# A macaron block on one core: the last squares summed on VectorE, the closing norm in pieces, and two VectorE differences moved in the mixer

## The chip, the cores and the metric

The kernel runs on one NeuronCore of a Trainium2 chip. The metric is the device time of one execution in microseconds. Three runs of the kernel before took 916.35, 917.20 and 917.82 us; the median is 917.2. The engines are TensorE (PE, with PEld for its weight loads), VectorE (DVE), ScalarE (ACT), GpSimd (POOL) and SyncE (SP), which issues most of the transfers. POOL issues those that add to what lies at their destination.

## What is computed

One layer: a half feed-forward, a token mixer, a second half feed-forward, and a closing RMS norm over 1024 features of 512 tokens, all in float32.

```python
def rmsnorm(x, g):
    x32 = x.astype(jnp.float32)
    y = x32 * lax.rsqrt(jnp.mean(x32 * x32, axis=-1, keepdims=True) + EPS)
    return (y * g.astype(jnp.float32)).astype(x.dtype)

def swiglu(x, w_gate, w_up, w_down):
    return (jax.nn.silu(x @ w_gate) * (x @ w_up)) @ w_down

x = x + 0.5 * swiglu(rmsnorm(x, ffn1_norm[layer]), ...)
x = x + token_mixer(rmsnorm(x, mix_norm[layer]), w_in[layer], w_out[layer], ...)
x = x + 0.5 * swiglu(rmsnorm(x, ffn2_norm[layer]), ...)
...
return rmsnorm(x, final_norm)
```

The token mixer projects to queries, keys and values, runs four heads of differential attention and eight heads of dilated attention, and projects back.

## The kernel before, in words

Activations lie transposed, features on the partitions: `x[0]` to `x[7]` are 128 features by 512 tokens each. A float32 product is made of three products of rounded parts: every operand is cast on ScalarE to a high half (a CAST row), and VectorE takes the rest (a subtraction that writes the low half); TensorE adds high by high, high by low and low by high (`mm3`, L141 to L143).

**The mixer** is a list of pieces of TensorE work ("chunks"), in the order `plan` = v0 q0 q1 v1 q2 q3 q4 v2 q5 q6 v3 q7, eight chunks for each name. `q0` to `q7` are the projections of eight attention units (units 0 to 3 differential, 4 to 7 dilated); each makes a query tile `pq` and a key tile `pk` in PSUM. Work of the other engines is put at a chunk with a rank: `put(t, rank, f)`. Ranks below 10 are emitted before the products of chunk `t`, ranks of 10 and more behind them; within one side smaller ranks come first. TensorE, VectorE and ScalarE execute in exactly the order in which the program was emitted, so these numbers set the order on each engine. SP and POOL are ordered by a scheduler.

When the projection of a unit is done (chunk `e`), its two tiles are scaled (`tq`, `tk`) and turned into score operands: `q0`, `q1` hold queries and their rests on the two halves of the partitions; `k0`, `k1` the keys, and `l0`, `l1` the rests of the keys. There are three ways. Units 0 and 7 are done at once (`evac_now`). Units 1 to 4 cast in `evac_q` at chunk `e`, and in `evac_k` at `e + 1` copy halves by SP's transfers, take the rests of the keys (L1051) and then the rests of the queries (L1054). Units 5 and 6 cast the whole key tile (`cast_k`, L1083), take its rest `kl` (`low_k`, L1089), and send both to the four places by four transfers each on SP's queue (`send`, L1078).

The attention of a unit starts some five chunks behind its projection. A score (`score`, L1191 and L1192) is two products into one of only two PSUM tiles tagged `s`; VectorE then adds the bias strip and finds the row's extreme in one custom instruction (L1194, `pr<-sc,strip`), which frees the PSUM tile, and ScalarE takes the exponential (L1197). For units 0 to 3 the finished head is turned, scaled into a high half `mh` (ScalarE, L1272) and a low half `ml` (VectorE, L1291), and POOL adds both into one tile `mx` by transfers (L1285, L1286). The weights of the projections are split as they come: cast on ScalarE (L916), rest on VectorE (L920).

**The end.** The second feed-forward closes with down projections by blocks: four units of seven steps (`SEVEN`), each step 12 products of 128 x 256, which yield two features' tiles at a time from sums and differences. In the last unit (`x[6]`, `x[7]`) the steps run as `LAST_SEVEN`: a11, s3, s2, a12, a22, s1, s4. Behind a step, `down_step` updates a half of `x[6]` or `x[7]` (L461), and `last` is called for the closing norm. The squares of `x[0]` to `x[5]` have been summed in `sq` before; the squares of `x[6]` and `x[7]` go to `q6`, `q7` (tiles `sql`) on ScalarE, by halves of 256 tokens (`left`, `right`).

The closing norm works by halves of the tokens. `final_means(hh)` takes the column means of the squares with 128 x 1 products (`st_n`, L1666), here over three sources (`sq`, `q6`, `q7`) and two blocks of 128 tokens; ScalarE takes the root (L1669), VectorE the reciprocal and a step of refinement (L1670 to L1674) and two diagonal tiles (`dgl`, L1677). `final_spread(hh)` spreads the factors over the partitions with one product (`bcl`, L1681), and `final_out` multiplies eight tiles (L1691) and sends them out in pairs on SP's queue. `final_end` runs at the last step: the spread of the left half, one pair of results, means and factors of the right half, the other three pairs, then the right half.

Of the kernel before, what the change touches and what calls it, by code (L numbers as in the profile page):

```python
# [21 lines left out]
P = 128  # L22
S = 512
# [59 lines left out]
def tile_macaron(ctx: ExitStack, tc, xs, xT, wf, wgu1, wst1, wd1, wdg1, wqk, wv, wo, wgu2, wst2, wd2,  # L83
# [922 lines left out]
    def qk_chunks(u):  # L1006
# [34 lines left out]
        def evac_k():  # L1041
            q0, q1, k0, k1, l0, l1 = qk[u]
            tq, tk = st["tq"], st["tk"]

            def other_half(t, a, b):
                nc.sync.dma_start(t[b, :].bitcast(F32), t[a, :].bitcast(F32))

            other_half(k0, lo, hi)
            other_half(k1, hi, lo)
            for a, b, kx, lx in ((lo, hi, k0, l0), (hi, lo, k1, l1)):  # L1050
                V.tensor_tensor(lx[a, :], tk[a, :], kx[a, :].bitcast(F32), op=ALU.subtract)  # L1051
                other_half(lx, a, b)
            for a, b, qx in ((lo, hi, q0), (hi, lo, q1)):
                V.tensor_tensor(qx[b, :], tq[a, :], qx[a, :].bitcast(F32), op=ALU.subtract)  # L1054
# [19 lines left out]
        elif u in SPREAD:  # L1074
# [28 lines left out]
            put(e + 2, 11, low_k)  # L1103
# [3 lines left out]
        else:  # L1107
            put(e, 11, evac_q)
            put(e + 1, 11, evac_k)
        return [lambda k=k: chunk(k) for k in range(KD)]  # L1110
# [531 lines left out]
    def last(t, o, put):  # L1642


        left, right = slice(0, HS), slice(HS, S)
        if o == "s3":
            fin["sq"] = [slot(4 + i, f"sql{i}") for i in range(2)]
        q6, q7 = fin["sq"]
        for name, n, q, c in (("a12", KD - 2, q6, left), ("a22", KD - 1, q7, left),
                              ("s1", KD - 1, q7, right), ("s4", KD - 2, q6, right)):  # L1650
            if o == name:
                put(t, A.activation, q[:, c], x[n][:, c], AF.Square)
        if o == "s3":
            put(t, A.activation, root[:], eps[:], AF.Sqrt)
        elif o == "s1":
            put(t, final_means, 0)
# [3 lines left out]
    def final_means(hh):  # L1660
        ps = pp.tile([P, S], F32, tag="mm", name=f"st_n4{hh}", bufs=4)
        n = NQ // 2
        for i in range(n):
            c = slice((hh * n + i) * P, (hh * n + i + 1) * P)
            for q, src in enumerate((sq, *fin["sq"])):
                T.matmul(ps[:, i:i + 1], src[:, c], ones_d[:, 0:1], start=q == 0, stop=q == 2)  # L1666
        y = sp.tile([P, n], F32, tag="yt4", name=f"ly{hh}", bufs=2)
        t = sp.tile([P, n], F32, tag="mx", name=f"lt{hh}", bufs=3)
        A.activation(y[:], ps[:, :n], AF.Sqrt, bias=eps[:])  # L1669
# [6 lines left out]
        for i in range(n):  # L1676
            V.tensor_scalar_mul(dg[:, i * P:(i + 1) * P], ident[:], y[:, i:i + 1])  # L1677

    def final_spread(hh):
        pb = fin["pb", hh] = pp.tile([P, S], F32, tag="mm", name=f"bcl{hh}", bufs=4)  # L1680
        T.matmul(pb[:, :HS], ones_m[:], fin["dg", hh][:, :HS], start=True, stop=True)  # L1681

    def final_out(hh, pairs):
        c = slice(hh * HS, (hh + 1) * HS)
        pb = fin["pb", hh]
        for g2 in pairs:
            y = cp.tile([P, S], F32, tag=f"xh{hh * 4 + g2}", name=f"y{hh}{g2}")
            y2 = y[:].rearrange("p (m q) -> p m q", m=2)
            for j in range(2):
                m = 2 * g2 + j  # L1690
                V.scalar_tensor_tensor(y2[:, j, :], x[m][:, c], sm[:, 3 * KD + m:3 * KD + m + 1],  # L1691
                                       pb[:, :HS], op0=ALU.mult, op1=ALU.mult)
                if hh == 1 and g2 == KD // 2 - 1:
                    nc.sync.dma_start(out[m * P:(m + 1) * P, c], y2[:, j, :])
            if hh == 0 or g2 < KD // 2 - 1:
                nc.sync.dma_start(
                    out[2 * g2 * P:(2 * g2 + 2) * P, c].rearrange("(m p) q -> p m q", p=P), y2)

    def final_end():
        final_spread(0)  # L1700
        final_out(0, range(1))
        final_means(1)
        final_out(0, range(1, 4))
        final_spread(1)
        final_out(1, range(4))
# [111 lines left out]
```

## Time and profile before

| | |
|---|---|
| median of three runs | 917.2 us (916.35 to 917.82) |
| the profiled execution | 916.25 us |
| its span, first to last instruction | 914.5 us |
| mean granted TensorE clock | 0.996 |
| VectorE busy | 758.5 us, 83% |
| ScalarE busy | 546.0 us, 60% |
| transfers | 147.39 MB, mean 161 GB/s |

How to read the rows that follow: a row of the timeline gives start and duration in us, the engine, the line of the kernel, the operation, output and inputs by the program's names, the shape, and how many instructions of the kind follow each other. In brackets stands how long the engine had been idle before, and what ended that. SPq is the queue of SyncE, on which an instruction only issues a transfer. Several rows of one matmul in float32 are its passes.

### The profile page before, as it was taken

Reading aid. Unit: us, or ns where it says so; the run is one execution under the profiler, and the core shown is the slowest. Engines: PE = TensorE matmul, PEld = TensorE weight load, DVE = VectorE, ACT = ScalarE, POOL = GpSimd, SP = SyncE. Lnnn points to the kernel's source line nnn. Section 1 sums busy time; section 2 is a strip of 40 time slices with the busy share of each in tenths; the row PEclk is TensorE's granted clock in tenths of the full one; section 3 lists DMA queues with packets and bytes.
Section 4 is the critical chain, followed back from the end, with each engine's and each line's share of the span. In section 5 each row is a group of like instructions: output and inputs, shape, how many; then the busy total and the mean of one; then the engine's idle time right before and its main releaser. Section 6 shows DMA issues by size and latency. Waiting matters only on the chain.

```text
span 914.5 us, 17685 instructions
## 1 busy us (share of the span) xinstructions
PE 901.4 (99%) x6565; PEld 844.2 (92%) x6565; DVE 758.5 (83%) x1601; ACT 546.0 (60%) x1149; POOL 112.4 (12%) x142
## 2 busy tenths in 40 slices
PE   9999999999999999999999999999999999999995
PEld 7889999999999998988979889889999899999995
DVE  7699997677998994779887859999899678798796
ACT  7356674455765764666756848456667345666462
POOL 1011101012103100000000320011110111220100
PEclk9999999999999999999999999999999999999998
DMA  8456756578758742446364674556673857984732
GB/s 277 114 161 151 175 138 180 141 202 214 196 150 206 198 148 73 115 131 162 102 178 121 187 156 112 169 159 150 171 210 93 218 146 192 221 203 123 199 112 92
DMA packets 66598, 147.39 MB, mean 161 GB/s; under 512 B 7712, under 2 KB 10016, under 8 KB 66512
## 3 DMA queue, kind: packets, MB, share of 16 engines
q1 hardware_dynamic: 48672, 113.29, 38.4%
q0 software_dynamic: 17840, 32.98, 22.0%
q8 instruction: 51, 0.84, 0.4%
q14 instruction: 35, 0.29, 0.1%
HBM read 137.28 MB, written 2.14 MB: 152 GB/s over the span
## 4 chain that ended last, share of the span: by engine, by line
PE 93%; DVE 4%; ACT 2%; DMA 1%; issue 1%; SPq 0%; DVEq 0%; ACTq 0%
PE pv L985 2%; PE pv L987 2%; PE pv L986 2%; PE po L1232 2%; PE pdb L142 1%; PE pda L142 1%; PE pda L143 1%; PE pdb L143 1%; PE pda L141 1%; PE pdb L141 1%; PE pga L143 1%; PE pua L143 1%; PE pua L142 1%; PE pua L141 1%; PE pga L141 1%; PE pga L142 1%
## 5 line engine op out<-in xcount | busy, mean ns | idle before, releaser
L1197 ACT ACTIVATE pr<-pr,small 128x128 f32<-128x128 f32 (+3 forms) x64 | 36.0, 563 | 37.5 <-DVE small L1194 37.0
L420 ACT CAST w<-s2b 128x512 fp32r<-128x512 f32 x52 | 32.4, 624 | 22.8 <-DVE s2b L402 22.5
L420 ACT CAST w<-s2a 128x512 fp32r<-128x512 f32 x48 | 29.9, 624 | 22.4 <-DVE s2a L402 21.6
L1194 DVE CUSTOM_DVE_ANT_0 pr<-sc,strip 128x128 f32<-128x128 f32 (+3 forms) x64 | 30.7, 485 | 11.2 <-PE sc L1192 11.0
L424 DVE TENSOR_TENSOR w<-s2b,w 128x512 fp32r<-128x512 f32 x52 | 35.7, 687 | 1.6 <-ACT w L420 1.1
L985 PE MATMUL pv<-w,xh 128*128 128x256 f32 x128 | 36.0, 282 | 0.0
L986 PE MATMUL pv<-w,xl 128*128 128x256 f32 x128 | 35.8, 280 | 0.0
L987 PE MATMUL pv<-w,xh 128*128 128x256 f32 x128 | 35.7, 279 | 0.0
L424 DVE TENSOR_TENSOR w<-s2a,w 128x512 fp32r<-128x512 f32 x48 | 33.0, 687 | 1.0 <-ACT w L420 0.7
L141 PE MATMUL pq<-xh,w 128*128 128x512 f32 x64 | 26.5, 414 | 0.0
L920 DVE TENSOR_TENSOR w<-raw_qk,w 128x512 fp32r<-128x512 f32 x32 | 21.6, 686 | 5.6 <-ACT w L916 5.6
L142 PE MATMUL pq<-xl,w 128*128 128x512 f32 x64 | 25.2, 393 | 0.0
L141 PE MATMUL pk<-xh,w 128*128 128x512 f32 x64 | 25.1, 392 | 0.0
L143 PE MATMUL pq<-xh,w 128*128 128x512 f32 x64 | 25.0, 391 | 0.0
L142 PE MATMUL pk<-xl,w 128*128 128x512 f32 x64 | 25.0, 391 | 0.0
L143 PE MATMUL pk<-xh,w 128*128 128x512 f32 x64 | 25.0, 391 | 0.0
L985 PEld LDWEIGHTS pv<-w,xh 128*128 128x128 f32 x128 | 24.1, 188 | 0.3
L986 PEld LDWEIGHTS pv<-w,xl 128*128 128x128 f32 x128 | 24.1, 188 | 0.2
L987 PEld LDWEIGHTS pv<-w,xh 128*128 128x128 f32 x128 | 24.1, 189 | 0.0
L916 ACT CAST w<-raw_qk 128x512 fp32r<-128x512 f32 x32 | 19.4, 615 | 7.3 <-issue 4.2
L1191 PE MATMUL sc<-k,q 128*128 128x256 f32 (+2 forms) x64 | 23.2, 363 | 0.4 <-DVE small L1194 0.4
L1232 PEld LDWEIGHTS po<-v,ptb 128*128 128x128 f32 x160 | 21.6, 191 | 1.7
(835 smaller groups left out, 4093.0 us busy)
## 6 DMA issues: line engine op xcount, KB each, us to landing
raw_qk<-wqk_dram SPq DMA_DIRECT2D x16, 512.0 KB, 3.4
raw0bg<-wst_dram SPq DMA_DIRECT2D x9, 512.0 KB, 4.3
raw0bu<-wst_dram SPq DMA_DIRECT2D x9, 512.0 KB, 5.5
raw_gua<-wgu_dram SPq DMA_DIRECT2D x8, 512.0 KB, 3.7
raw0ag<-wst_dram SPq DMA_DIRECT2D x8, 512.0 KB, 4.6
raw0au<-wst_dram SPq DMA_DIRECT2D x8, 512.0 KB, 5.4
raw0ad<-wdg_dram SPq DMA_DIRECT2D x8, 512.0 KB, 5.6
strip<-bias_rows SPq DMA_DIRECT2D x16, 256.0 KB, 4.0
```

The lines of the kernel that those rows point to most:

```text
L141: T.matmul(po, wh, mh, start=first, stop=False, skip_group_check=on)
L142: T.matmul(po, wh, ml, start=False, stop=False, skip_group_check=on)
L143: T.matmul(po, wl, mh, start=False, stop=last, skip_group_check=on)
L420: A.copy(made[t][0], source(t))
L424: V.tensor_tensor(l, source(t), h.bitcast(F32), op=ALU.subtract)
L985: T.matmul(po, xh[k][:, xs], wh[:, o:o + 256], start=k == 0, stop=False)
L986: T.matmul(po, xl[k][:, xs], wh[:, o:o + 256], start=False, stop=False)
L987: T.matmul(po, xh[k][:, xs], wl[:, o:o + 256], start=False, stop=k == KD - 1)
L1191: T.matmul(ps[:, :n], qs[:, qi], ks[:, :n], start=True, stop=False)
L1194: V.tensor_tensor_reduce(out=pi, in0=ps[:, :w], in1=st["b"][m][:, w - 1::-1], op0=ALU.add, op1=ALU.min, scale=1.0, scalar=3.0e38, accum_ou ...
L1197: A.activation(pi, pi, AF.Exp, scale=-1.0, bias=st["mx"][:, m, i:i + 1], accum_out=st["ls"][:, m, i:i + 1])
L1232: T.matmul(st["po3"][:, i, d0:d0 + dn], st["ptb", m, i][:, k * P:(k + 1) * P], vk, start=k == 0, stop=k == i)
```

## The change

In the mixer, the rests of the queries (L1054) leave `evac_k` and become `evac_rests`, put at chunk `e + 2` with rank 7 instead of the end of `e + 1`; this holds for units 1 to 4. For units 5 and 6, `low_k` stays at chunk `e + 2` but goes from rank 11 to rank 7, so that its subtraction and its four transfers are emitted before that chunk's products.

At the end, VectorE adds the left halves of the last squares into `sq`, so the means of the left half read `sq` alone. Means, root and factors are functions of their own. The means of the right half are taken in three pieces: of `sq` before the left half's spread, of `q7` and `q6` behind it. Three results of the left half come before the second factors instead of two, and five behind. The second diagonal of the right half is made on ScalarE. The spread is made in two halves of 128 columns.

```diff
@@ qk_chunks
                 V.tensor_tensor(lx[a, :], tk[a, :], kx[a, :].bitcast(F32), op=ALU.subtract)
                 other_half(lx, a, b)
+
+        def evac_rests():
+            q0, q1, k0, k1, l0, l1 = qk[u]
+            tq = st["tq"]
             for a, b, qx in ((lo, hi, q0), (hi, lo, q1)):
                 V.tensor_tensor(qx[b, :], tq[a, :], qx[a, :].bitcast(F32), op=ALU.subtract)
...
             put(e + 1, 6.7, cast_k)
-            put(e + 2, 11, low_k)
+            put(e + 2, 7, low_k)
...
             put(e, 11, evac_q)
             put(e + 1, 11, evac_k)
+            put(e + 2, 7, evac_rests)
@@ last
         if o == "s3":
             fin["sq"] = [slot(4 + i, f"sql{i}") for i in range(2)]
+            put(t, A.activation, root[:], eps[:], AF.Sqrt)
...
             if o == name:
+                if o == "s1":
+                    put(t, final_means, 0, (sq,))
+                    put(t, final_roots, 0)
                 put(t, A.activation, q[:, c], x[n][:, c], AF.Square)
-        if o == "s3":
-            put(t, A.activation, root[:], eps[:], AF.Sqrt)
-        elif o == "s1":
-            put(t, final_means, 0)
+                if c == left:
+                    put(t + 700, V.tensor_tensor, sq[:, c], sq[:, c], q[:, c], ALU.add)
+        if o == "s1":
+            put(t, final_factors, 0)
         elif o == "s4":
             put(t, final_end)
@@ final_factors (was the second part of final_means)
         for i in range(n):
-            V.tensor_scalar_mul(dg[:, i * P:(i + 1) * P], ident[:], y[:, i:i + 1])
+            if hh == 0 or i == 0:
+                V.tensor_scalar_mul(dg[:, i * P:(i + 1) * P], ident[:], y[:, i:i + 1])
+            else:
+                A.activation(dg[:, i * P:(i + 1) * P], ident[:], AF.Copy, scale=y[:, i:i + 1])
@@ final_spread
-        T.matmul(pb[:, :HS], ones_m[:], fin["dg", hh][:, :HS], start=True, stop=True)
+        for c in (slice(0, P), slice(P, HS)):
+            T.matmul(pb[:, c], ones_m[:], fin["dg", hh][:, c], start=True, stop=True)
@@ final_end
+        q6, q7 = fin["sq"]
+        final_means(1, (sq,), True)
         final_spread(0)
-        final_out(0, range(1))
-        final_means(1)
-        final_out(0, range(1, 4))
+        final_means(1, (q7, q6))
+        final_roots(1)
+        final_out(0, range(3))
+        final_factors(1)
+        final_out(0, range(3, KD))
         final_spread(1)
-        final_out(1, range(4))
+        final_out(1, range(KD))
```

The new `final_means(hh, srcs, more)` makes, for each source and each of two blocks of 128 tokens, one 128 x 1 product into the half's PSUM tile; `final_roots` is the root on ScalarE; `final_out` counts single results instead of pairs and sends them out as before.

What moves on the engines shows in the instruction order. First VectorE in the mixer, behind the projection of unit 3 (`l`, `q`: rests of keys and queries; the two ISA rows are one reduction of a score of unit 2 and the read of its row result; `w`: low half of weights). Before:

```order
L1051 TENSOR_TENSOR l_4987<-tk_4990,k_4985 64x512
L1051 TENSOR_TENSOR l_4988<-tk_4990,k_4986 64x512
L1054 TENSOR_TENSOR q_4983<-tq_4989,q_4983 64x512
L1054 TENSOR_TENSOR q_4984<-tq_4989,q_4984 64x512
L1194 ISA pr_4894,small_4896<-sc_5032,strip_4890 128x384
L1194 ISA small_4896 128x1
L920 TENSOR_TENSOR w<-raw_v_4925,w 128x512
```

And with the change:

```order
L1051 TENSOR_TENSOR l_4987<-tk_4990,k_4985 64x512
L1051 TENSOR_TENSOR l_4988<-tk_4990,k_4986 64x512
L1199 ISA pr_4894,small_4896<-sc_5030,strip_4890 128x384
L1199 ISA small_4896 128x1
L1058 TENSOR_TENSOR q_4983<-tq_4989,q_4983 64x512
L1058 TENSOR_TENSOR q_4984<-tq_4989,q_4984 64x512
L920 TENSOR_TENSOR w<-raw_v_4925,w 128x512
```

The reduction passes the two rests; what follows keeps its place. Unit 4's pair moves in the same way, unit 1's behind a reduction and the combination in front of it, and unit 2's keeps its place.

Second, VectorE behind the projection of unit 5 (`tx`: low half of turned weights of unit 4; `ml`: low half of head 3; `kl`: rest of unit 5's keys). Before:

```order
L1341 TENSOR_TENSOR mx_5656<-po_5534,lo_5657 64x512
L1320 TENSOR_TENSOR tx_5489<-pt_5671,tx_5489 128x384
L1291 SCALAR_TENSOR_TENSOR ml_5641<-ot_5635,few,mh_5640 128x512
L1089 TENSOR_TENSOR kl_5688<-tk_5621,kh_5650 128x512
L920 TENSOR_TENSOR w<-raw_v_5558,w 128x512 x2
```

With the change:

```order
L1346 TENSOR_TENSOR mx_5656<-po_5534,lo_5657 64x512
L1325 TENSOR_TENSOR tx_5489<-pt_5671,tx_5489 128x384
L1093 TENSOR_TENSOR kl_5678<-tk_5621,kh_5650 128x512
L1296 SCALAR_TENSOR_TENSOR ml_5641<-ot_5635,few,mh_5640 128x512
L920 TENSOR_TENSOR w<-raw_v_5558,w 128x512 x2
```

The two change places; for unit 6 the order is as it was.

Third, TensorE at the end, from the last product of the last unit's last step (`pydb`) on. Before:

```order
L143 MATMUL pydb_10746<-h1b_10263,w 128x256
L1681 MATMUL bcl_10875<-dgl_10858,ones_m 128x256
L1666 MATMUL st_n_10881<-few,sq 128x1
L1666 MATMUL st_n_10881<-few,sql_10779 128x1
L1666 MATMUL st_n_10881<-few,sql_10780 128x1
L1666 MATMUL st_n_10881<-few,sq 128x1
L1666 MATMUL st_n_10881<-few,sql_10779 128x1
L1666 MATMUL st_n_10881<-few,sql_10780 128x1
L1681 MATMUL bcl_10910<-dgl_10895,ones_m 128x256
```

With the change:

```order
L143 MATMUL pydb_10746<-h1b_10263,w 128x256
L1677 MATMUL st_n_10873<-few,sq 128x1 x2
L1703 MATMUL bcl_10876<-dgl_10856,ones_m 128x128 x2
L1677 MATMUL st_n_10873<-few,sql_10780 128x1 x2
L1677 MATMUL st_n_10873<-few,sql_10779 128x1 x2
L1703 MATMUL bcl_10909<-dgl_10896,ones_m 128x128 x2
```

The means of `sq` go ahead of the first spread; the others stay behind it, `q7` (sql_10780) first. Ahead of this stretch, two mean products of `sq` stand where six of three sources stood, between the steps s1 and s4.

49 lines of the change are left out of this document (29 added, 20 removed).

## The prediction

> **What bounds the kernel now.** I read the page first, then the list of who waited for whom on TensorE, and then the timeline of the stretches where those waits lie.
>
> ```profile
> span 914.5 us, 17685 instructions
> PE 901.4 (99%) x6565; PEld 844.2 (92%) x6565; DVE 758.5 (83%) x1601; ACT 546.0 (60%) x1149; POOL 112.4 (12%) x142
> PE bcl L1681 <- DVE dgl L1677: 1.9, 2, 1.7
> PE sc L1192 <- DMA l<-kl: 1.3, 1, 1.3
> PE sc L1191 <- DVE small L1194: 0.4, 1, 0.4
> ```
>
> TensorE is busy for 99% of the span, so time can only come from its few waits and from the stretch behind its last product. Two of the waits listed lie in the mixer, where the change moves VectorE work: a score that waits for a transfer (1.3 us) and one that waits for a VectorE reduction (0.4 us). The third is at the end, which the change rewrites. All three places are touched, and nothing else is.
>
> **First move: the query rests (units 1 to 4).** A score may not start before the reduction of the score two before it has freed its PSUM bank. For unit 3 the rows are, VectorE and then TensorE:
>
> ```profile
> 420.50 1.40 DVE L1054 TENSOR_TENSOR q<-tq,q 64x512 fp32r<-64x512 f32 x2
> 421.94 0.56 DVE L1194 CUSTOM_DVE_ANT_0 pr<-sc,strip 128x384 f32<-128x384 f32 x1
> 423.88 0.55 DVE L1194 CUSTOM_DVE_ANT_0 pr<-sc,strip 128x384 f32<-128x384 f32 x1
> 418.63 0.34 PE L1192 MATMUL sc<-l,q 128*128 128x384 f32 x1
> 421.56 0.39 PE L142 MATMUL pk<-xl,w 128*128 128x512 f32 x1
> 421.79 0.40 PE L143 MATMUL pk<-xh,w 128*128 128x512 f32 x1
> 422.56 0.50 PE L1191 MATMUL sc<-k,q 128*128 128x512 f32 x1 [0.38 <-DVE small L1194]
> 424.87 0.48 PE L1191 MATMUL sc<-k,q 128*128 128x512 f32 x1
> ```
>
> The scores were there at 418.97, yet the reduction stood behind two query rests of 1.40 us and ended at 422.50; TensorE went on 0.06 later. From start to start its product took 0.77 us where its neighbours stand 0.23 apart, so the stall is 0.54. With the rests behind the reduction, that runs at 420.50 and ends at 421.06, before TensorE asks at 422.02: the stall goes. What is late next is the following score. VectorE does the same sum of work up to 423.88, so its next reduction still ends at 424.43 and frees the bank at 424.49, while TensorE now asks at 424.87 - 0.54 = 424.33. It waits 0.16 there; 0.54 - 0.16 = **0.38** is left. Bounds: 0 if the backlog comes back whole, 0.54 if none of it does. Of the other three pairs, unit 2's keeps its place, and no wait of TensorE is listed at units 1 and 4, so I set them to 0. The scores that need the rests start four chunks of products later, which hides them; without that cover a pair would cost its 1.40 us.
>
> **Second move: the low half of the keys (unit 5).** Its product waits for the second of four transfers:
>
> ```profile
> 472.26 0.56 DVE L1320 TENSOR_TENSOR tx<-pt,tx 128x384 fp32r<-128x384 f32 x1 [0.34 <-ACT tx L1315]
> 472.73 0.74 DVE L1291 SCALAR_TENSOR_TENSOR ml<-ot,few,mh 128x512 fp32r<-128x512 f32 x1
> 473.39 0.68 DVE L1089 TENSOR_TENSOR kl<-tk,kh 128x512 fp32r<-128x512 f32 x1
> 473.77 0.85 POOL L1286 DMA_DIRECT2D mx<-ml  x1 [2.82 <-DVE ml L1291]
> 474.62 4.12 DMA l<-kl
> 477.33 0.28 PE L1191 MATMUL sc<-k,q 128*128 128x256 f32 x1
> 478.88 0.36 PE L1192 MATMUL sc<-l,q 128*128 128x256 f32 x1 [1.27 <-DMA l<-kl]
> l<-kl SPq DMA_DIRECT2D x2, 128.0 KB, 2.3
> ```
>
> TensorE idled 1.27 of the 1.55 us between the starts of the two products, and at most 0.28 of them is the first one's own work, so the stall lies between 1.27 and 1.55; I take the middle, 1.4, by which TensorE asks at 477.48. The change lets kl run ahead of ml: it starts at 472.73 instead of 473.39, 0.66 earlier, and all four transfers behind it on SP's queue with it. The awaited one is issued at 473.96. In the trace it took 4.12 us to land, and POOL's accumulating transfer mx<-ml was issued 0.85 us before it. The last row is the same kind of transfer one unit later, with no such neighbour: 2.3 us. Now ml is 0.60 later, so mx<-ml is issued near 474.4, behind the awaited transfer and not ahead of it. It lands at 476.3 with 2.3 us and at 478.1 with 4.12, and TensorE went on 0.14 after the landing at 478.74. The stall left is 0 in the first case and 0.75 in the second: gains of 1.4 and 0.65. I take **1.4**, since the awaited one is now ahead of its neighbour and nearest to the undisturbed row; even 3.3 us would do. The lower end for the range is 0.65; a loss would need a landing over 4.8 us, which no row of these transfers shows. The result ml is read by POOL's transfer alone; the differences that read its sum (L1125, in a row further down) start at 492.9 at the earliest, and that cover of 14 us would have to be gone before its 0.60 cost anything. Unit 6's low half keeps its place in the order, and so does everything on the queues of SP and POOL.
>
> [...]
>
> **The end.** Rows of the last unit in order of time:
>
> ```profile
> 897.67 0.42 DVE L461 SCALAR_TENSOR_TENSOR x<-pxdb,x 128x256 f32<-128x256 f32 x1 [0.95 <-PE pxdb L143]
> 898.12 0.42 ACT L449 ACTIVATE sql<-x 128x256 f32<-128x256 f32 x1 [0.96 <-DVE x L461]
> 898.72 0.30 PEld L1666 LDWEIGHTS st_n<-few,sq 128*128 128x128 f32 x2
> 899.03 0.42 DVE L461 SCALAR_TENSOR_TENSOR x<-pydb,x 128x256 f32<-128x256 f32 x1 [0.94 <-PE pydb L143]
> 899.64 0.58 PE L1666 MATMUL st_n<-few,sql 128*128 128x1 f32 x4
> 900.08 0.36 PE L141 MATMUL pydb<-h1b,w 128*128 128x256 f32 x1
> 900.26 0.26 ACT L1669 ACTIVATE ly<-st_n,few 128x2 f32<-128x2 f32 x1 [0.36 <-PE st_n L1666]
> 901.41 0.48 DVE L1677 TENSOR_SCALAR dgl<-ident,ly 128x128 f32<-128x128 f32 x2
> 901.95 0.70 PE L1681 MATMUL bcl<-dgl,ones_m 128*128 128x256 f32 x2 [0.19 <-DVE dgl L1677]
> 902.69 0.48 DVE L1691 SCALAR_TENSOR_TENSOR y<-x,bcl 128x256 f32<-128x256 f32 x1 [0.46 <-PE bcl L1681]
> 903.08 0.48 DVE L1691 SCALAR_TENSOR_TENSOR y<-x,x,bcl 128x256 f32<-128x256 f32 x1
> 904.04 0.26 ACT L1669 ACTIVATE ly<-st_n,few 128x2 f32<-128x2 f32 x1 [1.37 <-PE st_n L1666]
> 904.34 0.17 DVE L1670 RECIPROCAL ly<-ly 128x2 f32<-128x2 f32 x1 [0.78 <-ACT ly L1669]
> 905.20 0.48 DVE L1677 TENSOR_SCALAR dgl<-ident,ly 128x128 f32<-128x128 f32 x2
> 905.60 2.44 DVE L1691 SCALAR_TENSOR_TENSOR y<-x,x,bcl 128x256 f32<-128x256 f32 x6
> 908.34 2.83 DVE L1691 SCALAR_TENSOR_TENSOR y<-x,x,bcl 128x256 f32<-128x256 f32 x7
> L1125 DVE TENSOR_TENSOR mx<-mx x4: 411/422/425, 492.9 to 541.4; 128x256 f32<-128x256 f32 x4
> 441.08 0.35 ACT L1241 ACTIVATE ob<-po,small 128x128 f32<-128x128 f32 x1
> ```
>
> From 902.69 on VectorE sets the end: sixteen results 0.39 apart, the second factors, and one hole (903.47 to 904.34, 0.87) in which it waits for the second means. It ends at 908.34 + 2.83 = 911.17; the last transfer and the closing drain stand 3.3 us behind that and stay.
>
> The two added sums of 0.42 fall into VectorE's idle 0.95 and 0.94. The second is on the path: the square ends at 898.54, the sum at about 898.99, so TensorE's first mean starts near 899.05 instead of 898.72, 0.33 late. But two mean products replace six. Six took 898.72 to 900.06, or 0.22 each, so the last step starts at 899.05 + 0.45 = 899.50, 0.56 earlier. It also needs the update that ends at 899.45: just met. ScalarE's root follows at 899.69 (0.57 earlier), the diagonals are there by 901.32, and the last product ends in time for two means of sq ahead of the spread (0.45). The spread starts near 901.40 instead of 901.95, and so the first result is **0.55** earlier, at 902.14. Cutting it in two halves of 128 columns adds no columns, and ScalarE's table load, whose trigger the diff writes ahead of the squares' list, stays at its place in the order: both 0.
>
> Behind the spread, four mean products in place of six: 901.94 to 902.83, with the last square, 0.56 earlier too, there in time. The second root runs near 902.95 and ends at 903.21. The third result (902.92 to 903.40) now fills the hole, and the reciprocal follows at once: **0.87** gone. One of two second diagonals goes to ScalarE, which idles: VectorE saves half of 905.20 to 905.60, **0.20**; ScalarE's price from the last row is 0.35, under cover of five results (2 us). The sum is 0.55 + 0.87 + 0.20 = **1.62**. If the added sum and its two handovers took the whole lead, 1.07 is left; if the second means are late by a result too, 0.6. SP's queue holds only outputs there, in the old order.
>
> [...]
>
> **Sum.** 0.38 + 1.4 + 1.62 = 3.4 us. The profiled execution took 916.25 with its span of 914.5, so it would take 912.85; the median of the three runs, 917.2, lies 0.95 above it, and the forecast for the median is **913.8**. The gain of the mixer lasts to the end: behind it TensorE has one listed wait of 0.2, and the other engines follow its products.
>
> **Rivals.**
> - *The transfer stays slow* (4.12 us, sharing with mx<-ml): 0.38 + 0.65 + 1.62 = 2.65, so 914.5. For it: SP's four transfers and POOL's are still within a microsecond. Against: the order of issue turns round. 0.20.
> - *Only the end gains.* The mixer's 1.8 us are waits of one execution; VectorE's backlog or the transfers return them within the unit. 917.2 - 1.62 = 915.6, within 0.2%. For it: VectorE's 0.16 comes back at the very next score. Against: in the row below VectorE idled 1.96 us in front of the delayed score of unit 5, so at that point it carries no backlog that could take the time back. 0.12.
>
> ```profile
> 479.27 0.29 DVE L1194 CUSTOM_DVE_ANT_0 pr<-sc,strip 128x128 f32<-128x128 f32 x1 [1.96 <-PE sc L1192]
> ```
>
> - *Slower: weights late in the mixer.* Behind each of the three moved pairs stands a low half of weights (L920). If the reduction now ahead of the pair is not ready, VectorE stands still, and the weights come up to a pair later: 3 x 1.40 = 4.2, against the end's 1.62, so 919.8. It decides from where a low half ends after TensorE's first use of it. Against: the order has the same rows in front of those weights, the scores were ready 1.5 us before, and no wait for weights is listed. 0.06.
> - *The end does not gain* (the handovers from ScalarE over VectorE to TensorE are as long as four saved products): 0.38 + 1.4 + 0.6 = 2.4, so 914.8. 0.10.
>
> **How the numbers follow.** The forecast has 0.52. A measurement of this kernel can tell about 0.2%, 1.83 us, from no change. Faster by more: the forecast, the slow transfer and the last rival, 0.82, less 0.04 for runs that scatter by 0.7 around the median: 0.78. Within: 0.12 + 0.03 = 0.15. Slower: 0.07. The low end, 912.3, is the largest gain, 0.54 + 1.55 + 1.7 = 3.8, with 1.1 for scatter; the high end, 916.1, covers the case in which only the end gains, with 0.5.
>
> **What would show it.** Right: no wait of TensorE for l<-kl, or one under 0.2; the wait of 0.38 at the score replaced by one near 0.16; VectorE without a hole between its third result and the reciprocal; some 7.4 us from the first result to the last. Wrong: a landing of l<-kl over 3.5 us; the last step of the last unit starting less than 0.3 earlier against its fellow before it; a table load on ScalarE ahead of its diagonal; new waits of TensorE for weights behind the moved pairs.

## The result, and the profile after

The changed kernel takes **913.4 us** (median of 6 runs, 912.95 to 915.13) where the kernel before took 917.2 in the same rounds; the ratio on record is 0.9965, with an interval of 0.9955 to 0.9975; the two medians by themselves give 0.9959. The forecast was 913.8 with a range of 912.3 to 916.1, and faster.

The page of the changed kernel gives a span of 911.7 us and this busy time of each engine:

```profile
PE 900.5 (99%) x6561; PEld 842.8 (92%) x6561; DVE 758.7 (83%) x1602; ACT 546.3 (60%) x1150; POOL 112.6 (12%) x142
```

The list of TensorE's waits (us in total, times, longest) now has these two on top, beside one at the kernel's start that was there before:

```profile
PE bcl L1703 <- DVE dgl L1696: 1.6, 1, 1.6
PE po L1237 <- DVE ob L1266: 0.3, 1, 0.3
```

Nothing was taken off VectorE, which moved from 758.5 to 758.7. Both waits of scores are gone from the list. One wait is new, of products with the values (`po`) for VectorE's scaled rows (`ob`). The span is 2.8 us shorter, against a forecast sum of 3.4. To see where it went I set each product of TensorE beside its fellow in the kernel before and took the difference of the starts, the lead. It is 0.53 at unit 3's score (422), 0.30 two us later, 0.03 at 468, 1.56 behind unit 5's score (477), 1.60 at 498, 1.08 behind 542, and the same until the last unit; the end adds 1.69. Against the forecast's sum that is 0.35 less for the first move, 0.13 more for the second (1.56 less the 0.03 that was there), another 0.05 by 498, 0.53 given back, and 0.07 more at the end.

**First move.** TensorE's scores of unit 3, and VectorE's rows there, in the timeline of the changed kernel:

```profile
422.03 0.39 PE L1196 MATMUL sc<-k,q 128*128 128x512 f32 x1
424.58 0.50 PE L1196 MATMUL sc<-k,q 128*128 128x512 f32 x1
420.51 0.56 DVE L1199 CUSTOM_DVE_ANT_0 pr<-sc,strip 128x384 f32<-128x384 f32 x1
421.10 1.39 DVE L1058 TENSOR_TENSOR q<-tq,q 64x512 fp32r<-64x512 f32 x2
423.96 0.55 DVE L1199 CUSTOM_DVE_ANT_0 pr<-sc,strip 128x384 f32<-128x384 f32 x1
466.89 0.69 DVE L1262 TENSOR_TENSOR ob<-po,f 128x512 f32<-128x512 f32 x1
```

The reduction now stands ahead of the rests, and the score starts at 422.03 instead of 422.56, as said. VectorE starts the next reduction as late as before (423.96 and 423.88), so the next score starts only 0.29 earlier. The last row has this fellow in the timeline of the kernel before:

```profile
466.87 0.69 DVE L1257 TENSOR_TENSOR ob<-po,f 128x512 f32<-128x512 f32 x1
```

VectorE is at the same place at the same time in both kernels (466.89 and 466.87), while TensorE's lead is down to 0.03. VectorE gained nothing from the earlier score, so each handover from it to TensorE takes back a part of the lead.

**Second move.** VectorE, the issues on SP's queue and TensorE in unit 5's first score:

```profile
472.69 0.68 DVE L1093 TENSOR_TENSOR kl<-tk,kh 128x512 fp32r<-128x512 f32 x1
473.40 2.39 SPq L1082 DMA_DIRECT2D l<-kl  x4
474.33 0.85 POOL L1291 DMA_DIRECT2D mx<-ml  x1 [3.42 <-DVE ml L1296]
477.27 0.28 PE L1196 MATMUL sc<-k,q 128*128 128x256 f32 x1
477.39 0.28 PE L1197 MATMUL sc<-l,q 128*128 128x256 f32 x1
```

And from the view of the transfers (KB, us from issue to landing) the second of the four, whose issue runs at 473.95 and for which the score waits:

```profile
l<-kl SPq DMA_DIRECT2D x1, 128.0 KB, 2.5
```

The second product follows the first after 0.12: no wait is left. The transfer lands in 2.5, where it took 4.12. The last of the four, issued behind the neighbour `mx<-ml` (474.33), took 4.8: the slow landings are still there, but for transfers before which no wait is listed.

**What was given back.** VectorE and TensorE at unit 7's values, kernel before:

```profile
541.42 0.42 DVE L1125 TENSOR_TENSOR mx<-mx 128x256 f32<-128x256 f32 x1 [4.16 <-DMA mx<-ml]
542.73 1.89 PE L1232 MATMUL po<-v,ptb 128*128 128x64 f32 x16
```

ScalarE, GpSimd, VectorE and TensorE there, changed kernel:

```profile
527.55 0.59 ACT L1279 CAST mh<-ot 128x512 fp32r<-128x512 f32 x1 [0.20 <-PE ot L1273]
531.13 0.87 POOL L1474 DMA_DIRECT2D s2wo<-wo_dram  x1 [1.93 <-DMA s2wo<-wo_dram]
531.67 0.90 POOL L1290 DMA_DIRECT2D mx<-mh  x1
537.28 0.85 POOL L1291 DMA_DIRECT2D mx<-ml  x1 [4.71 <-issue]
540.47 0.42 DVE L1130 TENSOR_TENSOR mx<-mx 128x256 f32<-128x256 f32 x1 [4.81 <-DMA mx<-ml]
540.81 0.61 DVE L1266 TENSOR_TENSOR ob<-po,small 128x192 f32<-128x192 f32 x2
541.57 1.97 PE L1237 MATMUL po<-v,ptb 128*128 128x64 f32 x16 [0.28 <-DVE ob L1266]
```

VectorE's first difference of the mixer (`mx<-mx`) stands ahead of unit 7's scale (`ob`) and reads unit 6's whole output, which GpSimd's accumulating transfer `mx<-ml` completes (`mx<-mh` writes the tile, `mx<-ml` adds to it). VectorE idles 4.81 for it. From the start of the difference to TensorE's next values it is 541.57 - 540.47 = 1.10. In the kernel before the same row stood at 541.42, which allows TensorE 542.52, and TensorE came at 542.73: there were 0.21 of cover. In the changed kernel TensorE is 1.6 earlier and the difference only 0.95, so the cover is used up. TensorE's next products are then 1.08 to 1.16 ahead instead of 1.59; the ends of products are modelled, which is why the wait itself reads only 0.28.

The rows also show where the difference lost the lead. Unit 6's high half `mh` is there 1.61 earlier than before (528.14 against 529.75). But GpSimd first issues two transfers of weights (`s4wo`, `s2wo`), and idles before each until an earlier transfer has landed, so `mx<-mh` is issued 3.53 behind `mh`, only 1.21 earlier than before. It took 4.9 us to land, where it took 4.5; `mx<-ml` is issued 0.7 behind that landing in both kernels. No version was run that issues `mx<-mh` ahead of the weights.

**The end.** VectorE's rows, with the start of the last step on TensorE ahead of them:

```profile
898.43 0.37 PE L141 MATMUL pydb<-h1b,w 128*128 128x256 f32 x1
900.98 0.48 DVE L1713 SCALAR_TENSOR_TENSOR y<-x,bcl 128x256 f32<-128x256 f32 x1 [0.41 <-PE bcl L1703]
902.16 0.16 DVE L1688 RECIPROCAL ly<-ly 128x2 f32<-128x2 f32 x1
903.22 2.04 DVE L1713 SCALAR_TENSOR_TENSOR y<-x,x,bcl 128x256 f32<-128x256 f32 x5
905.57 2.83 DVE L1713 SCALAR_TENSOR_TENSOR y<-x,x,bcl 128x256 f32<-128x256 f32 x7
```

The last step starts 1.65 earlier than before (900.08), 0.57 beyond the mixer's 1.08. No idle time stands ahead of the second reciprocal, which follows the third result. From first result to last end it takes 908.40 - 900.98 = 7.42, where it took 911.17 - 902.69 = 8.48.

### The profile page after: what moved, and what is told of

It is laid out like the page before. It is cut to its first block, busy times and chain, and to the rows that moved or that the text cites. A ratio compares the mean times of both kernels' runs of the same rounds, so it can differ in the third digit from the quotient of the medians.

```text
span 911.7 us, 17678 instructions
## 1 busy us (share of the span) xinstructions
PE 900.5 (99%) x6561; PEld 842.8 (92%) x6561; DVE 758.7 (83%) x1602; ACT 546.3 (60%) x1150; POOL 112.6 (12%) x142
## 4 chain that ended last, share of the span: by engine, by line
PE 96%; DVE 2%; DMA 1%; ACT 1%; issue 1%; SPq 0%; DVEq 0%; ACTq 0%
PE po L1237 2%; PE pv L985 2%; PE pv L986 2%; PE pv L987 2%; PE pq L141 2%; PE pq L142 2%; PE pk L141 2%; PE pq L143 2%; PE pk L142 2%; PE pk L143 2%; PE pdb L142 1%; PE pda L141 1%; PE pdb L141 1%; PE pda L142 1%; PE pda L143 1%; PE pdb L143 1%
```

## The experiments

Spans are of the one profiled execution, medians of all runs of a kernel. The changed kernel in the first row was measured beside the kernel before at 917.2. The others ran in three groups (rows 2 to 5, 6 to 9 and 10 to 13), in which the kernel before had medians of 916.2, 917.0 and 916.8. The ratios are those on record and not quotients of the medians; the two differ by up to 0.001, so differences of less than a microsecond are read from the traces. Numbers in brackets count the runs.

| kernel | span | median | ratio to before |
|---|---|---|---|
| changed kernel | 911.7 | 913.39 (6) | 0.9965 [0.9955, 0.9975] |
| first move undone | 911.4 | 913.46 (10) | 0.9965 [0.9952, 0.9978] |
| second move undone | 913.1 | 914.77 (12) | 0.9985 [0.9975, 0.9995] |
| unit 6 copied by ScalarE | 912.5 | 913.92 (6) | 0.9969 [0.9957, 0.9980] |
| before, unit 3 copied by ScalarE | 913.3 | 915.16 (12) | 0.9991 [0.9980, 1.0002] |
| unit 6 added by VectorE | 914.0 | 913.04 (5) | 0.9967 [0.9954, 0.9979] |
| mixer moves alone | 916.4 | 915.21 (11) | 0.9988 [0.9977, 0.9999] |
| three sources for the left means | 912.6 | 914.39 (1) | |
| two results ahead | 911.7 | 913.46 (1) | |
| both diagonals on VectorE | 911.8 | 913.56 (1) | |
| added on VectorE, both diagonals on ScalarE | 910.7 | **912.47** (5) | 0.9954 [0.9942, 0.9967] |
| the same, two results on GpSimd | 912.9 | 914.41 (8) | 0.9971 [0.9961, 0.9981] |
| changed kernel again | 911.8 | 913.40 (5) | 0.9962 [0.9948, 0.9976] |

### The first move undone

```diff
-            put(e + 2, 7, evac_rests)
+            put(e + 1, 11, evac_rests)
```

> The changed kernel with its first mixer move alone undone: the query rests of units 1 to 4 stand ahead of the next reduction again. Forecast's step: the stall of 0.54 at unit 3's score is back, the later wait of 0.16 is gone, so this run is 0.38 slower than the changed kernel (span 912.1). Reading of the two traces: the stall of about 0.5 comes back at unit 3's score, but by the score of unit 4's time (468) TensorE stands where it stood with the move, because VectorE and ScalarE run the same chain at the same times; the span is 911.7 to 911.8 and the lead over the changed kernel at 468 is under 0.1.

The wait is back in TensorE's list, with its old size:

```profile
PE sc L1196 <- DVE small L1199: 0.4, 1, 0.4
```

Against the changed kernel, TensorE is 0.54 later than it was ahead of the score (0.60 at 422.03 less 0.06 that it was late at 400 already), 0.30 at 424.58, 0.15 at 437 and 0.03 at 468, by the same subtraction. The medians, 913.46 against 913.39, can't decide on 0.38, since the median of the kernel before differs by 0.9 between the two groups. By the traces the reading holds and the forecast's 0.38 falls: the move is worth nothing here. That its span is 0.3 below the changed kernel's has its cause at 541, where the transfer of unit 6 landed sooner in this execution (`mx<-mx` at 540.06) and TensorE did not wait.

### The second move undone

```diff
-            put(e + 2, 7, low_k)
+            put(e + 2, 11, low_k)
```

> The changed kernel with its second mixer move alone undone: unit 5's low half of the keys stands behind unit 3's low half of the output again. Forecast's step: the score of unit 5 waits for its transfer 1.3 to 1.4 and all of it stays, so this run is 1.4 slower (span 913.1). Reading of the two traces: the stall is back with 1.3 to 1.5, but the wait of 0.28 at unit 7's values (541) is gone, since TensorE then comes there later than the accumulating transfer of unit 6 ends; 1.1 slower than the changed kernel (span 912.8).

Unit 5's score in the timeline, and its transfer in the chain that ended last (start, us, what):

```profile
479.07 0.35 PE L1197 MATMUL sc<-l,q 128*128 128x256 f32 x1 [1.30 <-DMA l<-kl]
```

```profile
474.79 4.14 DMA l<-kl
```

The stall is back. Against the changed kernel TensorE loses 1.46 at this product and 1.53 at the next (1.68 and 1.75, with 0.22 ahead of the score). At 541 it gets 0.52 of it back, since the new wait of `po` is gone from the list. That is the pattern of the reading: 1.5, then less. Behind 542 it is 1.26 later, 1.04 net of the 0.22, which is nearer to the reading's 1.1 than to the forecast's 1.4. The span, 1.4 longer, and the medians don't tell the two apart; the lead along the trace does.

### Unit 6's whole output by a copy

```diff
-            if u == 5:
+            if u in (5, 6):
                 A.copy(w[:], st["ot"][:])
                 return
```

> The changed kernel, with unit 6's whole output made by one ScalarE copy from PSUM, as unit 5's is, in place of two GpSimd transfers (the copy holds the value before its split in two, not the sum of the two parts). Theory from the traces: VectorE's first difference of the mixer waits 4.8 for the accumulating transfer and delays the scale of unit 7 behind it; with the copy that wait goes, so does the wait of 0.28 of unit 7's values at 541, and the mixer's gain of 1.56 reaches the end: span 911.2 to 911.3, 0.4 to 0.5 under the changed kernel. Rival: the wait at 541 is VectorE's or ScalarE's backlog of work and not the transfer; then the copy of about 0.7 on ScalarE makes it later, and the span is 911.7 to 912.2.

VectorE's wait for the transfer is gone, and so is TensorE's at 541. But two new waits stand ahead of it, in this kernel's timeline of TensorE:

```profile
530.22 0.33 PE L1220 MATMUL pt<-ident,pr 128*128 128x128 f32 x1 [0.36 <-ACT ptb L1226]
```

The second is 0.11, at 533.37, for the copy itself. Until the copy has run (532.75 to 533.31 on ScalarE) unit 6's transposed output occupies one of the two PSUM banks from which `pt` is taken, and the transposes have the other alone. TensorE loses 0.89 at these two places and gets 0.52 back at 541. The wait at 541 was the transfer's, but this way of removing it costs more than it: the median is 913.92. Neither expectation had that.

### The kernel before, with unit 3's output by a copy

```diff
+            if u == 3:
+                A.activation(w[:], st["ot"][:], AF.Copy, scale=sub8[:])
+                return
```

> The kernel before, with unit 3's whole output made by one ScalarE copy from PSUM in place of two GpSimd transfers; unit 5's low half of the keys is as late as before. Neighbour theory: the keys' transfer took 4.12 from issue to landing because the accumulating transfer of 256 KB ran beside it; without that it lands in 2.5 or less, and unit 5's score waits 0 to 0.2 (span 913.2 to 913.5). Rival, position theory: the transfer takes about 4 whatever runs beside it, or the copy makes the keys' split later by its 0.7; the wait of about 1.3 stays or grows (span 914.3 to 915.2). The lateness of kl alone: if the transfer took 3.4 as a middle case, a wait of 0.6 is left.

Here `kl` is nearly as late as it was before, behind `ml`, and unit 3's two transfers on GpSimd's queue are missing; the one beside the keys was `mx<-ml`. VectorE and TensorE in its timeline:

```profile
473.25 0.68 DVE L1089 TENSOR_TENSOR kl<-tk,kh 128x512 fp32r<-128x512 f32 x1
477.31 0.28 PE L1192 MATMUL sc<-l,q 128*128 128x256 f32 x1
```

The second transfer, whose issue runs at 474.6, in the view of the transfers:

```profile
l<-kl SPq DMA_DIRECT2D x1, 128.0 KB, 2.3
```

The transfer lands in 2.3 and the score doesn't wait, though `kl` starts only 0.14 earlier than in the kernel before. So the stall was the neighbour's doing: 256 KB of accumulation beside the keys' transfers (4.12 with it, 2.3 without), and not the 0.66 by which the keys stood behind `ml`. The lead grows by 1.51 behind this score (from 0.13 to 1.64), as with the move (1.53), and 0.6 of it is lost at 541 here too, in a wait for the same scale that reads 0.35: what is given back there belongs to whatever brings TensorE forward and not to the move's new order.

### Unit 6's whole output by VectorE, in the gap

```diff
+            if quick and i == NQ - 1:
+                put(s + step * i + 1, 5.5, lambda: V.tensor_tensor(
+                    whole[6][:], mh[6][:].bitcast(F32), ml[6][:].bitcast(F32), op=ALU.add))
...
+            if u == 6:
+                return
```

> The changed kernel, with unit 6's whole output made by one VectorE addition of its two parts (128x512, about 0.7), behind unit 7's last reciprocal, where VectorE stood idle for 4.3 to 4.9 before its first difference; the two GpSimd transfers of that unit are gone, and ScalarE and its PSUM bank are left alone. Transfer theory: the wait before the first difference is gone, unit 7's scale runs as soon as its values are there, no wait of TensorE at 541; the lead of 1.56 that the second move brought reaches the next stage, and the span is 911.2 to 911.4, 0.3 to 0.5 under the changed kernel. Rival, backlog theory: VectorE is late there by its own work; 0.7 more of it moves the scale later, and the span is 911.7 to 912.4.

VectorE's rows at unit 7, the addition first:

```profile
538.38 0.67 DVE L1383 TENSOR_TENSOR mx<-mh,ml 128x512 f32<-128x512 f32 x1
541.86 0.62 DVE L1266 TENSOR_TENSOR ob<-po,small 128x192 f32<-128x192 f32 x2 [2.35 <-PE po L1237]
```

VectorE now waits for TensorE's values instead of a transfer, and TensorE's wait at 541 is gone; TensorE gains 0.52 on the changed kernel there. The profiled execution itself is long for another reason, in a stretch that the edit doesn't touch: from 232 to 284 TensorE ran 435 products where the changed kernel ran 462. The other four executions have spans of 911.0 to 912.3, and the median is 0.35 under the changed kernel's, inside both intervals. The transfer theory holds by the trace.

### The mixer's moves alone

The end of the kernel before, both moves of the change.

> The kernel before with the two mixer moves alone; the end is as before. By the forecast's terms it gains 0.38 + 1.4 = 1.8 on the kernel before (span 912.7); by the reading of the traces 1.56 at unit 5's score less 0.3 to 0.5 at 541, so 1.1 (span 913.4), with the end's last results 12.3 to 12.4 behind the start of its last step's products, as before.

The median is 915.21 beside 917.0, the ratio's interval allows gains of 0.1 to 2.1 us, so the times don't decide between 1.1 and 1.8. The profiled execution shows the wait at 541 in another size. GpSimd, VectorE and TensorE in its timeline:

```profile
533.03 0.90 POOL L1290 DMA_DIRECT2D mx<-mh  x1
542.04 0.43 DVE L1130 TENSOR_TENSOR mx<-mx 128x256 f32<-128x256 f32 x1 [6.59 <-DMA mx<-ml]
543.14 1.08 PE L1237 MATMUL po<-v,ptb 128*128 128x64 f32 x8 [2.05 <-DVE ob L1266]
```

Two windows behind that wait (stretch, length, busy time and count of PE, PEld, DVE, ACT and POOL, granted clock, DMA share, GB/s):

```profile
543.00:545.00 2.00, 1.86 (x17) 1.89 (x17) 0.00 (x0) 0.00 (x0) 0.00 (x0) 1.00 1.04 153
545.00:549.00 4.00, 4.00 (x15) 3.24 (x14) 1.59 (x5) 0.59 (x1) 0.86 (x1) 0.57 0.29 38
```

GpSimd issued `mx<-mh` 1.36 later than in the changed kernel, although `mh` was there 0.20 earlier: in front of the two weight transfers ahead of it GpSimd idled 5.06 and 2.61, where it idled 4.15 and 1.93. The same 1.10 lies between difference and values, and TensorE waited 2.05. Two us later the granted clock fell, and the products from 545 to 549 lost another 1.5. The end is as before: from the start of the last step to the end of the last result it takes 11.08, where it took 11.09. Eight profiles here have TensorE come early to 541 with the transfer in place: two had no wait, and the others 0.20 to 2.05. The three kernels with the addition on VectorE had none, nor had the one with the copy, nor the two in which TensorE comes late.

### The end, piece by piece

Means of the left half over three sources, without VectorE's sums:

```diff
-                    put(t, final_means, 0, (sq,))
+                    put(t, final_means, 0, (sq, q6, q7))
...
-                if c == left:
-                    put(t + 700, V.tensor_tensor, sq[:, c], sq[:, c], q[:, c], ALU.add)
```

> The changed kernel, with VectorE's two additions of squares in the left half left out and its means taken over three sources again (the same sums, made by TensorE). Forecast's step: the last step's products start 0.5 to 0.6 later behind the longer row of means, so do the first result and the end (span 912.2 to 912.3). Rival: TensorE's small products wait for the ScalarE square of the left half or overlap others, so that the additions bring only 0.2 or less.

TensorE's first product of the last step, behind the means of the left half:

```profile
899.28 0.36 PE L141 MATMUL pydb<-h1b,w 128*128 128x256 f32 x1
```

The last step starts 0.85 later than in the changed kernel, of which 0.29 were there since 541: 0.56 are the sums' worth, the forecast's very number. This and the next two rest on one execution each.

Two results ahead of the second factors:

```diff
-        final_out(0, range(3))
+        final_out(0, range(2))
...
-        final_out(0, range(3, KD))
+        final_out(0, range(2, KD))
```

> The changed kernel, with two results instead of three ahead of the second factors. Third-result theory: VectorE ends its second result about 901.85, and the root is there at about 901.95 to 902.05, since the right half's means are taken in pieces: a hole of 0.2 to 0.4 before the second reciprocal, and the right half's path (reciprocal, factors, diagonals, spread) starts 0.1 to 0.2 earlier, which buys nothing since the sixth to eighth results cover it: the end moves by the hole, 0.1 to 0.4 later (span 911.8 to 912.1). Rival: the means in pieces fill the whole hole by themselves, and the span stays 911.7.

```profile
900.64 0.48 DVE L1713 SCALAR_TENSOR_TENSOR y<-x,bcl 128x256 f32<-128x256 f32 x1 [0.47 <-PE bcl L1703]
901.72 0.17 DVE L1688 RECIPROCAL ly<-ly 128x2 f32<-128x2 f32 x1 [0.21 <-ACT ly L1682]
905.53 2.82 DVE L1713 SCALAR_TENSOR_TENSOR y<-x,x,bcl 128x256 f32<-128x256 f32 x7
```

In VectorE's rows a hole of 0.21 is back, and first result to last end takes 7.71, 0.29 more than 7.42. The span equals the changed kernel's only because this execution had no wait at 541. So of the old hole of 0.87 the third result closed 0.2 to 0.3. The other 0.6 are gone with two results ahead as well; that leaves the means in pieces, which no run took back alone.

Both diagonals of the right half on VectorE:

```diff
-            if hh == 0 or i == 0:
+            if True:
```

> The changed kernel, with both diagonals of the right half on VectorE. Forecast's step: VectorE's row from second reciprocal to fourth result is longer by one diagonal, so 0.2 more (1.06 becomes 1.26, as before the change), and the end 0.2 later. Rival: the right half's spread is what the ninth result waits for, and the diagonal on ScalarE brings nothing or loses: then the end does not move.

VectorE's rows in the order of time:

```profile
900.88 0.48 DVE L1713 SCALAR_TENSOR_TENSOR y<-x,bcl 128x256 f32<-128x256 f32 x1 [0.47 <-PE bcl L1703]
902.06 0.16 DVE L1688 RECIPROCAL ly<-ly 128x2 f32<-128x2 f32 x1
903.31 2.04 DVE L1713 SCALAR_TENSOR_TENSOR y<-x,x,bcl 128x256 f32<-128x256 f32 x5
905.66 2.83 DVE L1713 SCALAR_TENSOR_TENSOR y<-x,x,bcl 128x256 f32<-128x256 f32 x7
```

From the reciprocal to the next result it takes 1.25 instead of 1.06, and from first result to last end 7.61: 0.19 for one diagonal.

### Two versions beyond the change

The first is the changed kernel with unit 6 added on VectorE and with both diagonals of the right half on ScalarE (`if hh == 0:`).

> The changed kernel with unit 6's whole output added on VectorE (as in add6) and both diagonals of the right half on ScalarE. By the readings: the wait at 541 gone (0.3 to 0.5), one more diagonal of 0.2 off VectorE, whose results cover the later spread; span 911.0 to 911.2, 0.5 to 0.7 under the changed kernel. Rival: the second diagonal on ScalarE brings the spread behind the last left result, and only add6's gain is left (911.3).

```profile
900.26 0.48 DVE L1718 SCALAR_TENSOR_TENSOR y<-x,bcl 128x256 f32<-128x256 f32 x1 [0.47 <-PE bcl L1708]
901.44 0.16 DVE L1693 RECIPROCAL ly<-ly 128x2 f32<-128x2 f32 x1
902.18 2.04 DVE L1718 SCALAR_TENSOR_TENSOR y<-x,x,bcl 128x256 f32<-128x256 f32 x5
904.13 0.48 DVE L1718 SCALAR_TENSOR_TENSOR y<-x,bcl 128x256 f32<-128x256 f32 x1
904.53 2.83 DVE L1718 SCALAR_TENSOR_TENSOR y<-x,x,bcl 128x256 f32<-128x256 f32 x7
```

Reciprocal to fourth result is down to 0.74, the ninth result (904.13) doesn't wait for the later spread, and first result to last end takes 7.10: 0.32 under the changed kernel, more than the 0.2 expected. TensorE has no wait at 541 and gains 0.52 there. The span of 910.7 flatters it: TensorE was 0.36 ahead of the changed kernel's trace before 541 already. Its median, 912.47, is the lowest here, 0.93 under that of the changed kernel beside it; the intervals of the two ratios overlap.

The second gives two of the left half's results to GpSimd, which multiplies by a ScalarE copy of the spread:

```diff
+            A.activation(pbs[:, j * HS:(j + 1) * HS], fin["pb", 0][:, :HS], AF.Copy,
+                         scale=sm[:, 3 * KD + m:3 * KD + m + 1])
...
+            if hh == 0 and m >= KD - 2:
+                G.tensor_tensor(y2[:, j, :], x[m][:, c], fin["pbs"][:, j * HS:(j + 1) * HS], op=ALU.mult)
```

> As best_a, with two of the left half's eight results on GpSimd from a ScalarE copy of the spread that carries the weights of the last norm. Theory: the end is bound by VectorE's row of sixteen results; two fewer take 0.8 off it, if the right half's spread is there in time: span 910.2 to 910.6. Rival: GpSimd's products of 128x256 take over 1.5 each or slow VectorE's, and the gain is under 0.3 or a loss.

ScalarE, GpSimd, and VectorE's first result:

```profile
901.63 0.83 ACT L1738 ACTIVATE pbs<-bcl,x 128x256 f32<-128x256 f32 x2
902.18 1.41 POOL L1719 TENSOR_TENSOR y<-x,pbs 128x256 f32<-128x256 f32 x2 [29.66 <-ACT pbs L1738]
902.49 0.48 DVE L1721 SCALAR_TENSOR_TENSOR y<-x,bcl 128x256 f32<-128x256 f32 x1 [2.22 <-ACT pbs L1738]
```

The loss that the rival named came, but not for its reason, and the theory missed. GpSimd's products are cheap, 0.70 each. But VectorE's first result waits 2.22 until ScalarE has read the spread (901.63 + 0.83 = 902.46), where it waits 0.47, for TensorE's spread, in the version without: both engines read one PSUM tile (`bcl`), and here VectorE comes second. ScalarE makes its copies behind the second root, so from 901.63 only. Whether both could read the tile at the same time, no run here shows. That row is 2.23 later than in the version without, of which 0.44 is TensorE's, which starts its last step that much later and was 0.49 behind at 395 already. Nor did the row of results get shorter: from first result to last end it takes 7.06, beside 7.10, since the ninth result now idles 0.65 for the right half's spread. Copies ahead of the second root, copies that read the tile behind VectorE's results, or a spread made twice, were not tried.

The changed kernel itself ran beside these three.

> The changed kernel unchanged, on the chip of the three runs beside it, as their yardstick. Reading of the traces: the wait of unit 7's values at 541 hangs on where the transfer of unit 6 lands and so differs from run to run (0 to 0.9 in the profiles so far); spans 911.2 to 912.2.

It had a wait of 0.20 at 541, and its spans go from 911.1 to 912.5, a little wider than expected. That fits a wait that hangs on a transfer; only one of these executions was profiled.

## Why the prediction was right, point by point

- **The score of unit 3, 0.38.** The stall of 0.54 went, and the next score gave back 0.24 where 0.16 was said. The step failed behind that: "0.54 - 0.16 = 0.38 is left" counted one handover, and the later ones took the rest: 0.14 is left at 437, 0.03 at 468. Undoing the move costs nothing. It is the lower bound that the text named, 0 if the backlog comes back whole. VectorE does the same work in the same time, so the new order within it moved a wait and didn't shorten it.
- **The score of unit 5, 1.4.** The mechanism was right: the neighbour's transfer made it 4.12, and in front of it the transfer took 2.5, nearer to the 2.3 that the forecast preferred. The term was somewhat small: 1.53 from before to after, and 1.53 when the move was undone. The rival of the slow transfer (0.65) did not come. One reading beside it was wrong without a price: `ml` is read not by the transfer alone but also by TensorE's output projection (`pwo<-ml`), whose first row stands near 521, under even more cover.
- **"The gain of the mixer lasts to the end."** This step failed, with 0.5 of the 1.6. The prediction looked through TensorE's list for waits that were there. It had the right row in hand, the differences `mx<-mx` from 492.9 to 541.4, and took its first time for unit 3 without asking what the last one waits for. It waited 4.16 for a transfer, with 0.21 of cover for TensorE behind it. That "the other engines follow its products" holds for ScalarE, which had `mh` ready 1.61 earlier, and not for GpSimd, whose transfers stand one behind another and behind those of weights: its chain ended 0.95 earlier only. The rival in which only the end gains had a give-back, and named the transfers beside VectorE's backlog, but it had them return the whole gain within the unit.
- **The end, 1.62.** It measured 1.69. The last step's start 0.57 beyond the mixer's lead (forecast 0.56, 0.56 by the run with three sources), the first result 0.63 (0.55), the hole all of its 0.87, one diagonal 0.19 (0.20). The rival in which it doesn't gain falls with the run of three sources. The diagonal takes 0.40 on ScalarE and frees only 0.19 of VectorE, and it pays, since VectorE is the engine with no time to spare there: from first result to last end it takes 7.10 with two diagonals on ScalarE, 7.42 with one and 7.61 with none.
- **Weights late in the mixer.** No new wait of TensorE for weights in the mixer is in any list. This rival didn't come.
- **The sum.** 0.38 + 1.4 + 1.62 = 3.4 became 0.03 + 1.53 + 0.05 - 0.53 + 1.69 = 2.77 in span. The median fell by 3.8, a microsecond more than the span of the profiled executions: that of the kernel before lay 0.95 under its median, that of the changed kernel 0.13 above. In the last group the median fell by 3.4. That the forecast for it was off by 0.4 only is luck to that extent.

## What to carry to other kernels

When a stall goes, list every later place where an engine waits for something that does not follow the engine you made faster, transfers above all, and write beside each how much cover it has, and what stands ahead of it in its queue: the smallest cover caps the gain. An order changed within an engine that is late by its own work moved a wait here and paid nothing (0.54 less at the score, 0.03 left at 468); ask for the neighbour on another queue first, since removing an accumulating transfer did as much as moving the work (1.51 beside 1.53). Where one engine sets the end, small pieces of its row can go to an engine with time, even a slower one (a diagonal took 0.40 on ScalarE and freed 0.19 of VectorE), while their result stays under cover; a PSUM tile that both read cost more than it brought (VectorE's first result waited 2.22 in place of 0.47, and its row of results was shorter by 0.04).

## What was not expected of the hardware

One wait of 2.05 us cost 3.8. After it, in the run of the mixer's moves alone, the granted clock was 1.00 for two us and 0.57 on the mean of 545 to 549, and products of `pwo` came 0.43 apart, where 0.23 is usual. Waits of 1.30 (second move undone) and 0.93 (three sources) had no such sequel. The length of the wait alone doesn't decide: with the first move undone TensorE waited 1.63 ahead of the second spread at the end (903.01), the granted clock was 0.59 from 902 to 903 and 0.50 from 903 to 904, and the spread took 1.22; in the changed kernel the same wait of 1.63 left the clock at 1.00 up to 905, and the spread took 0.71. VectorE's results covered that. So the drop came behind 2.05 idle us in one run and within a wait of 1.63 in another; what sets it off, no run here shows. Whether the other long runs of the kernel with the mixer's moves have the same cause is open, for only this execution of it was profiled.

A transfer of 256 KB within the core on GpSimd's queue (`mx<-mh`, issued at 531 to 533) took 4.2 to 5.1 us to land in the ten traces that have it. That scatter of 0.9 is larger than the 0.21 of cover that the schedule had for the chain behind it.
